# Evacuations issued ahead of side streams, attention jobs over 19 points, and sample heads in bursts of two

## The chip, the cores and the metric

One core of one Trainium2 chip runs the whole program. The metric is the device time of one execution in microseconds; the time before is the median of three runs. A core has TensorE (PE in the profile; its weight loads are PEld), VectorE (DVE), ScalarE (ACT), GpSimd (POOL) and SyncE (SP), each of which works through its own list of instructions in order; semaphores tie the lists together. One profiled execution gives start and length of every instruction.

## What is computed

One layer of a streaming encoder over 640 tokens: 512 of a prompt, and 8 samples of 16 tokens each. The reference, cut to what matters here:

```python
z = x @ w_in                                   # xa | ya | glu | q | three gates
xa, ya, glu, q, gates = split(z)
h = rg_lru(causal_conv4([state_conv_a, xa]))   # sigmoid, exp, sqrt, scan
out_a = (h * gelu(ya)) @ proj_a
u = glu[..., :512] * sigmoid(glu[..., 512:])
v = causal_depthwise_conv31([state_conv_b, u])
out_b = silu(layer_norm(v, over 512 channels)) @ proj_b
out_c = softmax(q k^T / sqrt(128)) v @ proj_c  # 4 heads, 256 memory tokens;
                                               # the samples use cache_mem_k / cache_mem_v
merged = g0 * out_a + g1 * out_b + g2 * out_c  # g = sigmoid(gates)
x = layer_norm(alpha * x + merged @ w_out)
x = layer_norm(alpha * x + (silu(x @ w_ffn_gate) * (x @ w_ffn_up)) @ w_ffn_down)
```

All matrices are float32.

## The kernel before

**Tiling.** Activations lie transposed: channels on the 128 partitions, 640 tokens along the free dimension, handled as two halves of 320 (`HT`). A float32 product is made of three rounded ones: high part by high part, high by low, low by high. So every weight tile is copied by ScalarE into a rounded high part (`wh`), and VectorE subtracts to get the low part (`wl`); activations have `xh`, `xl`, or two `s` tiles made in the same way.

**Steps.** The program is a list of steps (`Step`). One with 8 blocks of the inner dimension is 48 matmuls of 128x320 for one block of 128 output channels; one with 4 blocks (`proj_b`, `proj_c`) is 24. Each writes two PSUM buffers named `pu`, of which there are four, so a step reuses the buffers of an earlier step and has to wait until that step's result has been evacuated (copied, or combined, into SBUF by ScalarE or VectorE: the step's `evac`). Two more, `pv`, serve the side work. The sequence is: keys and values of the memory; GLU gates and values, four blocks of each, with four queries in their middle; eight `xa`; eight of the gate of branch C; eight `proj_c`; then four times two of the gate of branch B and two `proj_b`; eight `ya`; the products of branch A and its gate (`pairs`, through `seven`, which forms sums of blocks first); `w_out`; and the feed-forward part.

**Side streams.** Work that isn't a step is written as generators: `attn` (cross-attention of the prompt, `attn_prompt`, then of the samples, `attn_sample`), `b` (the 31-wide convolution `conv_b_stream`, then the layer norm `ln_b_stream`), `lru`, `a`, and sums for the pairs. `advance` runs pieces of them, and issues more as long as a model of VectorE and ScalarE says that they have less queued than TensorE. Because each engine takes its instructions in the order in which the program issued them, what `advance` has issued stands in front of whatever is issued later.

**The main loop.** Each step's matmuls come in a few groups with a yield behind each. The evacuation of the step before is not issued at once but put in `pending`; at the next step's yields the loop calls `advance` and then `flush`, which issues what is pending (lines 1905 to 1912).

**Attention.** `attn_prompt` lists its jobs (transposes, scores, softmax in two parts, values) at 13 points; a `yield` separates them. `attn_sample` forms the scores of one head at a time (16 matmuls, from the cache tiles `kc`), each at a point of its own; the softmax then multiplies each head by the reciprocal of its row sums (`softmax_end`) before the transposes; the values (32 matmuls a head, tiles `vc`) again come one head at a time, and one copy of 128x512 takes them out. The cache is loaded by DMAs that GpSimd issues (L997).

**GpSimd.** It adds up the four channel blocks for the layer norm of branch B, twice (L782 and L784), and sets to zero the tiles into which the samples' queries (L916) and probabilities (L1032) are written.

**The GLU values.** The first three GLU steps form a group: their first halves of the tokens are done while the last tokens are still being prepared, then the second halves follow (`x_step`). There, in `fm`, the products of one block follow each other: high-high, high-low (which reads `xl`), low-high.

Of the kernel before, what the change touches and what calls it, by code (L numbers as in the profile page):

```python
# [143 lines left out]
def trunk(ctx, tc, x_prompt, x_sample, mem_t, rows_a, rows_b, hist_b, cache_k, cache_v, ln_in_g, ln_in_b, w_in,  # L144
# [484 lines left out]
    def fm(p, w, rh, rl, K, cs=(0, 1), apart=False):  # L629
        hi, lo = w  # L630
        if apart:
            for a, b in ((hi, rh), (hi, rl), (lo, rh)):
                for k in range(K):
                    for c in cs:
                        P.matmul(p[c][:, :HT], a[:, k], b(k, c), start=(k == 0 and a is hi and b is rh),
                                 stop=(k == K - 1 and a is lo))
                yield b is rl
            return
# [27 lines left out]
    def x_step(ld, o, evac, group=None):  # L666

        def mm(w):
# [4 lines left out]
            if group[1][0] is s:  # L673
                until(lambda: {0, 1, 2} <= turned)
                for z, q in enumerate(group[1]):
# [3 lines left out]
                    for n, few in enumerate(fm(q.p, q.w, xrh, xrl, KD, (0,), z in (0, 2))):  # L679
# [6 lines left out]
            yield from fm(s.p, w, xrh, xrl, KD, (1,))  # L686
# [92 lines left out]
    def ln_b_stream():  # L779
        def total(x):  # L780
            y = get([128, T])
            G.tensor_tensor(y, x[0], x[1], op=OP.add)  # L782
            for k in range(2, KC):
                G.tensor_tensor(y, y, x[k], op=OP.add)  # L784
# [91 lines left out]
    def attn_prompt():  # L876
# [35 lines left out]
        def queries(_):  # L912

            qs = qv["s"] = [get([128, NH, 128]) for _ in range(2)]
            for e in range(2):
                G.memset(qs[e], 0.0)  # L916
# [49 lines left out]
        for jobs in (((k_turn, 0),), ((k_split, 0), (scores, 0)), ((soft_a, 0), (scores, 1)), ((soft_b, 0), (soft_a, 1)),  # L966
                     ((turn, 0), (soft_b, 1), (scores, 2)), ((turned_split, 0), (soft_a, 2), (turn, 1)),
                     ((turned_split, 1), (soft_b, 2), (scores, 3)), ((soft_a, 3), (values, 0), (turn, 2)),
                     ((queries, 0), (values_split, 0), (turned_split, 2), (soft_b, 3)), ((turn, 3),),
                     ((turned_split, 3),), ((values, 1),), ((values_split, 1),)):  # L970
# [16 lines left out]
    def attn_sample():  # L987
# [25 lines left out]
        for h in range(NH):  # L1013
            yield None
            scores(h)
            if h + 2 < NH:
                load(kc, cache_k, h + 2)
            if h == NH - 1:
                load(vc, cache_v, 0)
            yield 1  # L1020
        free(*qs)
        pr = softmax_start(acc)
        yield 1
        load(vc, cache_v, 1)
        yield None
        pr = softmax_end(*pr)
        yield 1
        yield None
        pT = [[get([128, 4, 128]) for _ in range(2)] for _ in range(2)]
        for e in range(2):  # L1030
            for i in range(2):
                G.memset(pT[e][i], 0.0)  # L1032
# [11 lines left out]
        for h in range(NH):  # L1044
# [8 lines left out]
            if h + 2 < NH:  # L1053
                load(vc, cache_v, h + 2)
            yield 1
            yield None
# [4 lines left out]
        copy(o, p[:, 0])  # L1061
# [937 lines left out]
```

## Time and profile before

| | us |
|---|---|
| median of three runs (1058.47, 1059.86, 1059.86) | 1059.86 |
| the profiled execution | 1059.77 |
| its span in the profile | 1058.0 |
| PE busy | 1041.5 |
| DVE busy | 801.6 |
| ACT busy | 495.9 |
| POOL busy | 96.0 |

The span is what the profile covers from the first to the last instruction; the 1.8 us between it and the execution's own time lie around it. An engine that is busy 98% of the span, as PE is, isn't necessarily fast all that time: its matmuls are pipelined, and a matmul that starts late, or runs at a lower granted clock, counts as busy. Times of rows are microseconds from the span's start.

### The profile page before, as it was taken

The numbers are of one execution on the slowest core, as the hardware profiler recorded it, in microseconds if no ns is written. First come the engines' busy times: TensorE is split into PE (matmuls) and PEld (weight loads), VectorE is DVE, ScalarE is ACT, GpSimd is POOL, SyncE is SP. The second block draws the span as 40 slices with busy tenths as digits, with TensorE's granted clock in tenths as the row PEclk, the third lists the DMA queues.
The fourth block names the chain that finished last, engine by engine and source line by source line (L and its number), as shares of the span: only waits on it lengthen the run. The fifth ranks groups of instructions, "written<-read, shape, count | busy, mean of one in ns | idle before, by whom it ended". The sixth has DMA issues, their size and how long they took to land.

```text
span 1058.0 us, 16736 instructions
## 1 busy us (share of the span) xinstructions
PE 1041.5 (98%) x6689; PEld 986.7 (93%) x6689; DVE 801.6 (76%) x1400; ACT 495.9 (47%) x892; POOL 96.0 (9%) x164
## 2 busy tenths in 40 slices
PE   9999999999999999999999999999999999999997
PEld 6899899899999999999998899999999999888886
DVE  5769889799566746889586569888888887576775
ACT  5723564345674538555332355444444434434350
POOL 0000313223000000000211210000000000100111
PEclk9999999999999999999999999999999999999999
DMA  9722236512121122212735331222222222833471
GB/s 350 245 88 81 75 112 227 188 42 81 40 97 64 61 80 80 86 40 80 259 140 199 127 114 40 94 106 80 81 80 81 82 99 105 309 136 126 179 278 40
DMA packets 29854, 128.89 MB, mean 122 GB/s; under 512 B 4016, under 2 KB 4848, under 8 KB 19920
## 3 DMA queue, kind: packets, MB, share of 16 engines
q1 hardware_dynamic: 21168, 99.59, 26.5%
q0 software_dynamic: 8608, 28.23, 7.6%
q8 instruction: 52, 0.85, 0.3%
q14 instruction: 26, 0.21, 0.1%
HBM read 115.31 MB, written 12.50 MB: 121 GB/s over the span
## 4 chain that ended last, share of the span: by engine, by line
PE 83%; DVE 9%; ACT 3%; DMA 2%; issue 1%; POOL 0%; SPq 0%; DVEq 0%; ACTq 0%; POOLq 0%
PE pu L64 73%; PE pv L64 9%; DVE s L64 7%; ACT s L64 2%; DVE wl L64 1%; ACT L64 1%; DMA s<-in_w_mem_k 1%; DMA n<-s 1%; DMA s<-in_w_mem_v 1%; DVE xres L64 0%; ACT wh L64 0%; DMA s<-in_x_prompt 0%; DVE mx L64 0%; POOL s L784 0%; DVE xl L64 0%
## 5 line engine op out<-in xcount | busy, mean ns | idle before, releaser
L64 PE MATMUL pu<-xh,wh 128*128 128x320 f32 x1040 | 246.9, 312 | 3.5 <-ACT s L64 2.6
L64 PE MATMUL pu<-xh,wl 128*128 128x320 f32 x1040 | 244.3, 310 | 0.0
L64 ACT ACTIVATE wh<-wr 128x1024 fp32r<-128x1024 f32 (+1 forms) x149 | 134.9, 908 | 231.7 <-PE pu L64 138.7
L64 PE MATMUL pu<-xl,wh 128*128 128x320 f32 x888 | 216.6, 310 | 1.4 <-DVE xl L64 1.4
L64 PE MATMUL pu<-s,wh 128*128 128x320 f32 x1064 | 185.5, 310 | 1.8 <-DVE s L64 1.3
L64 DVE TENSOR_TENSOR s<-s,s 128x640 f32<-128x640 f32 (+5 forms) x200 | 141.8, 728 | 57.1 <-ACT s L64 54.8
L64 PEld LDWEIGHTS pu<-xh,wh 128*128 128x128 f32 x1040 | 176.5, 189 | 7.8 <-ACT s L64 3.8
L64 PEld LDWEIGHTS pu<-xh,wl 128*128 128x128 f32 x1040 | 176.9, 189 | 0.3 <-ACT s L64 0.3
L64 DVE TENSOR_TENSOR wl<-wr,wh 128x1024 fp32r<-128x1024 f32 (+1 forms) x113 | 129.8, 1151 | 62.3 <-ACT wh L64 62.1
L64 PEld LDWEIGHTS pu<-s,wh 128*128 128x128 f32 x1064 | 163.2, 188 | 3.2 <-ACT wh L64 1.1
L64 PEld LDWEIGHTS pu<-xl,wh 128*128 128x128 f32 x888 | 152.9, 189 | 1.8 <-DVE xl L64 1.8
L64 PE MATMUL pu<-s,wl 128*128 128x320 f32 x808 | 146.8, 309 | 0.0
L64 ACT ACTIVATE s<-s 128x640 fp32r<-128x640 f32 (+4 forms) x148 | 89.9, 627 | 96.4 <-DVE s L64 90.1
L64 DVE TENSOR_TENSOR s<-s,pu 128x320 f32<-128x320 f32 x188 | 88.6, 485 | 56.6 <-PE pu L64 52.9
L64 PEld LDWEIGHTS pu<-s,wl 128*128 128x128 f32 x808 | 125.6, 188 | 0.2 <-issue 0.2
L64 DVE SCALAR_TENSOR_TENSOR s<-s,pb,s 128x511 f32<-128x511 f32 (+14 forms) x240 | 114.5, 551 | 9.5 <-ACT s L64 9.4
L64 PE MATMUL pu<-wh,s 128*128 128x512 f32 x364 | 107.0, 383 | 0.0
L64 PEld LDWEIGHTS pu<-wh,s 128*128 128x128 f32 x364 | 66.9, 188 | 13.8 <-ACT wh L64 0.6
L64 ACT ACTIVATE s<-pu 128x320 f32<-128x320 f32 (+2 forms) x90 | 36.6, 441 | 65.3 <-PE pu L64 65.2
L64 PE MATMUL pu<-s,s 128*128 128x512 f32 (+1 forms) x236 | 61.9, 413 | 0.0
L64 PE MATMUL pu<-wl,s 128*128 128x512 f32 x182 | 57.1, 381 | 0.0
L64 PEld LDWEIGHTS pu<-s,s 128*128 128x128 f32 x236 | 43.1, 190 | 14.1 <-issue 7.1
(127 smaller groups left out, 1133.3 us busy)
## 6 DMA issues: line engine op xcount, KB each, us to landing
wr<-in_w_in SPq DMA_DIRECT2D x26, 1024.0 KB, 4.8
wr<-in_w_ffn_down SPq DMA_DIRECT2D x19, 1024.0 KB, 4.9
wr<-in_w_ffn_gate SPq DMA_DIRECT2D x11, 1024.0 KB, 4.8
wr<-in_w_ffn_up SPq DMA_DIRECT2D x11, 1024.0 KB, 4.7
s<-in_cache_k POOLq DMA_DIRECT2D x16, 256.0 KB, 5.6
s<-in_cache_v POOLq DMA_DIRECT2D x16, 256.0 KB, 4.9
wr<-in_proj_a SPq DMA_DIRECT2D x4, 1024.0 KB, 6.7
wr<-in_w_out SPq DMA_DIRECT2D x4, 1024.0 KB, 5.2
```

Source lines behind the costliest of these rows:

```text
L64: return f(*a, **k)
```

## The change

It has six parts.

1. **The main loop** calls `flush` before `advance`: a finished step's evacuation is issued before side work at the same yield.
2. **`attn_prompt`** spreads the same jobs over 19 points.
3. **`attn_sample`**: two heads' scores at one point, and two heads' values at one point; the loads of the cache move with them. The probabilities are no longer multiplied by the reciprocals; the copy of the result takes each head's reciprocal as its scale, in four pieces of 128x128.
4. **GpSimd to VectorE**: the block sums of `ln_b_stream`, and the memsets of the queries and probabilities.
5. **`fm`** gets a second order for a step that is done in turns: all high-high products, then all low-high ones of the weights, then those that need `xl`. The first step of the group uses it for its second half of tokens.
6. **`seven`**: the first pair forms the sums for the product `s1` at its second step instead of right before that product.

```diff
-    def fm(p, w, rh, rl, K, cs=(0, 1), apart=False):
+    def fm(p, w, rh, rl, K, cs=(0, 1), apart=None):
         hi, lo = w
         if apart:
-            for a, b in ((hi, rh), (hi, rl), (lo, rh)):
+            turns = ((hi, rh), (hi, rl), (lo, rh)) if apart == "w" else ((hi, rh), (lo, rh), (hi, rl))
+            for i, (a, b) in enumerate(turns):
                 for k in range(K):
                     for c in cs:
-                        P.matmul(p[c][:, :HT], a[:, k], b(k, c), start=(k == 0 and a is hi and b is rh),
-                                 stop=(k == K - 1 and a is lo))
-                yield b is rl
+                        P.matmul(p[c][:, :HT], a[:, k], b(k, c), start=(k == 0 and i == 0), stop=(k == K - 1 and i == 2))
+                yield i == 1
...
-                    for n, few in enumerate(fm(q.p, q.w, xrh, xrl, KD, (0,), z in (0, 2))):
+                    for n, few in enumerate(fm(q.p, q.w, xrh, xrl, KD, (0,), "w" if z in (0, 2) else None)):
...
-            yield from fm(s.p, w, xrh, xrl, KD, (1,))
+            yield from fm(s.p, w, xrh, xrl, KD, (1,), "x" if s is group[1][0] else None)
...
     def ln_b_stream():
         def total(x):
             y = get([128, T])
-            G.tensor_tensor(y, x[0], x[1], op=OP.add)
+            V.tensor_tensor(y, x[0], x[1], op=OP.add)
             for k in range(2, KC):
-                G.tensor_tensor(y, y, x[k], op=OP.add)
+                V.tensor_tensor(y, y, x[k], op=OP.add)
...
-                G.memset(qs[e], 0.0)
+                V.memset(qs[e], 0.0)
...
-        for jobs in (((k_turn, 0),), ((k_split, 0), (scores, 0)), ((soft_a, 0), (scores, 1)), ((soft_b, 0), (soft_a, 1)),
-                     ((turn, 0), (soft_b, 1), (scores, 2)), ((turned_split, 0), (soft_a, 2), (turn, 1)),
...
+        for jobs in (((k_turn, 0),), ((k_split, 0),), ((scores, 0),), ((soft_a, 0), (scores, 1)), ((soft_b, 0), (soft_a, 1)),
+                     ((turn, 0),), ((turned_split, 0), (soft_b, 1), (scores, 2)), ((soft_a, 2),), ((turn, 1),),
...
     def attn_sample():
-        for h in range(NH):
-            yield None
-            scores(h)
-            if h + 2 < NH:
-                load(kc, cache_k, h + 2)
-            if h == NH - 1:
-                load(vc, cache_v, 0)
+        for h in range(0, NH, 2):
+            for _ in range(2 if h else 1):
+                yield None
+            for i in range(2):
+                scores(h + i)
+            for i in range(2):
+                if h == 0:
+                    load(kc, cache_k, h + 2 + i)
+                elif i >= 0:
+                    load(vc, cache_v, i - 0)
             yield 1
         free(*qs)
-        pr = softmax_start(acc)
+        pr, sm = softmax_start(acc)
         yield 1
-        load(vc, cache_v, 1)
+        rc = small.tile([128, NH], F32, name="rc")
+        V.reciprocal(rc, sm)
         yield None
-        pr = softmax_end(*pr)
-        yield 1
+        yield None
         yield None
         pT = [[get([128, 4, 128]) for _ in range(2)] for _ in range(2)]
...
-                G.memset(pT[e][i], 0.0)
+                V.memset(pT[e][i], 0.0)
...
             free(*vc[h])
-            if h + 2 < NH:
-                load(vc, cache_v, h + 2)
-            yield 1
-            yield None
+            if h % 2:
+                if h == 1:
+                    load(vc, cache_v, 2)
+                    load(vc, cache_v, 3)
+                yield 1
+                for _ in range(2 if h == 1 else 1):
+                    yield None
...
-        copy(o, p[:, 0])
+        for h in range(NH):
+            hs = slice(h * 128, (h + 1) * 128)
+            A.activation(o[:, hs], p[:, 0, hs], AF.Copy, scale=rc[:, h:h + 1])
...
-            if first and xn[0] == "s":
+            if first and i == 1:
+                before = lambda: sums_for("s1")
+            elif first and xn[0] == "s":
                 before = lambda xn=xn: sums_for(xn)
...
             while new and s.wait:
                 new.pop(0).prep_lo()
+            flush()
             advance()
-            flush()
             while new:
                 new.pop(0).prep_lo()
```

Where the instructions stand now, at three places. The rows are a list of ScalarE's instructions in program order: operation, output, input and shape; `x2` is the same row twice. The number at the end of a name tells tiles apart, and differs between the two programs.

First, ScalarE from the middle of the GLU steps on, before. `s_83_1310<-pu` is the evacuation of the last GLU gate; `pv,nm` are the exponentials of a softmax (`soft_a`), `rc` its division (`soft_b`), `wh` the weights of a later step.

```order
L64 ACTIVATE wh<-wr 128x1024
L64 ACTIVATE s_78_1231<-s_78_1231,rc 128x256 x2
L64 ACTIVATE s_79_1232<-s_79_1232,rc 128x256 x2
L64 ACTIVATE s_81_1300,sm<-pv,nm 128x256 x2
L64 ACTIVATE s_82_1301,sm<-pv,nm 128x256 x2
L64 ACT_TABLE_LOAD
L64 ACTIVATE s_83_1310<-pu 128x320 x2
L64 ACTIVATE wh<-wr 128x1024
```

The same place of the changed program, where that evacuation is `s_81_1289<-pu`:

```order
L64 ACTIVATE wh<-wr 128x1024
L64 ACT_TABLE_LOAD
L64 ACTIVATE s_81_1289<-pu 128x320 x2
L64 ACTIVATE s_79_1237<-s_79_1237,rc 128x256 x2
L64 ACTIVATE s_80_1238<-s_80_1238,rc 128x256 x2
L64 ACT_TABLE_LOAD
L64 ACTIVATE s_82_1303,sm<-pv,nm 128x256 x2
L64 ACTIVATE s_83_1304,sm<-pv,nm 128x256 x2
L64 ACTIVATE wh<-wr 128x1024
```

The evacuation, with the table load that belongs to it, now stands ahead of both softmax pieces, and a second table load ahead of the exponentials.

Second, ScalarE at the first two steps of the gate of branch B, before. `lru` marks the exponentials of the recurrence, the row behind each pair is a square; `pu,pa` are the sigmoids that evacuate a gate's step; `s_190_2988<-s_190_2988` is the first of four square roots.

```order
L64 ACTIVATE s_216_3525<-s_211_3370,lru_88 128x640
L64 ACTIVATE s_211_3370<-s_211_3370,lru_88 128x640
L64 ACTIVATE s_192_3011<-s_216_3525 128x640
L64 ACTIVATE wh<-wr 128x512
L64 ACT_TABLE_LOAD
L64 ACTIVATE s_217_3561<-pu,pa 128x320 x2
L64 ACT_TABLE_LOAD
L64 ACTIVATE s_190_2988<-s_190_2988 128x640
```

The same of the changed program:

```order
L64 ACT_TABLE_LOAD
L64 ACTIVATE s_215_3547<-pu,pa 128x320 x2
L64 ACT_TABLE_LOAD
L64 ACTIVATE s_216_3565<-s_203_3326,lru_88 128x640
L64 ACTIVATE s_203_3326<-s_203_3326,lru_88 128x640
L64 ACTIVATE s_181_2900<-s_216_3565 128x640
L64 ACTIVATE wh<-wr 128x1024
L64 ACT_TABLE_LOAD
L64 ACTIVATE s_217_3585<-pu,pa 128x320 x2
```

The sigmoids now stand between groups of exponentials, with a table load on each side, where they stood behind all of them. Over the whole program ScalarE has 24 table loads instead of 21.

Third, ScalarE at the samples' softmax, before; `s_151_2374<-pu` evacuates an `xa` step.

```order
L64 ACTIVATE s_140_2300<-s_83_1310,pb 128x640
L64 ACTIVATE wh<-wr 128x1024
L64 ACTIVATE s_145_2354,sm<-pv,nm 128x256 x2
L64 ACTIVATE s_146_2355,sm<-pv,nm 128x256 x2
L64 ACTIVATE s_151_2374<-pu 128x320 x2
```

The same of the changed program:

```order
L64 ACTIVATE s_141_2328<-s_81_1289,pb 128x640
L64 ACTIVATE s_150_2398,sm<-pv,nm 128x256 x2
L64 ACTIVATE s_151_2399,sm<-pv,nm 128x256 x2
L64 ACTIVATE wh<-wr 128x1024
L64 ACT_TABLE_LOAD
L64 ACTIVATE s_152_2441<-pu,pa 128x320 x2
```

The exponentials used to stand directly ahead of the evacuation of an `xa` step; now they stand, with a weight copy and a table load, ahead of the evacuation of the first step of the gate of branch C (`pu,pa`), and the multiplication by `rc` that followed them is gone: it is in the four copies behind the values.

More of the change, by code (lines that the diff above doesn't have):

```diff
@@ L965, in attn_prompt @@
         matmuls = (k_turn, scores, turn, values)
-        for jobs in (((k_turn, 0),), ((k_split, 0), (scores, 0)), ((soft_a, 0), (scores, 1)), ((soft_b, 0), (soft_a, 1)),
-                     ((turn, 0), (soft_b, 1), (scores, 2)), ((turned_split, 0), (soft_a, 2), (turn, 1)),
-                     ((turned_split, 1), (soft_b, 2), (scores, 3)), ((soft_a, 3), (values, 0), (turn, 2)),
-                     ((queries, 0), (values_split, 0), (turned_split, 2), (soft_b, 3)), ((turn, 3),),
-                     ((turned_split, 3),), ((values, 1),), ((values_split, 1),)):
+        for jobs in (((k_turn, 0),), ((k_split, 0),), ((scores, 0),), ((soft_a, 0), (scores, 1)), ((soft_b, 0), (soft_a, 1)),
+                     ((turn, 0),), ((turned_split, 0), (soft_b, 1), (scores, 2)), ((soft_a, 2),), ((turn, 1),),
+                     ((turned_split, 1), (soft_b, 2), (scores, 3)), ((soft_a, 3),), ((values, 0),),
+                     ((values_split, 0), (soft_b, 3), (turn, 2)), ((turned_split, 2),), ((turn, 3), (queries, 0)),
+                     ((turned_split, 3),), (), ((values, 1),), ((values_split, 1),)):
             for f, i in jobs:
```

## Prediction

> **What bounds the kernel now.** I read the page first: busy shares and the chain that ended last.
>
> ```profile
> span 1058.0 us, 16736 instructions
> PE 1041.5 (98%) x6689; PEld 986.7 (93%) x6689; DVE 801.6 (76%) x1400; ACT 495.9 (47%) x892; POOL 96.0 (9%) x164
> PE 83%; DVE 9%; ACT 3%; DMA 2%; issue 1%; POOL 0%; SPq 0%; DVEq 0%; ACTq 0%; POOLq 0%
> ```
>
> TensorE is busy 98% of the span and is 83% of the chain. The change leaves its set of matmuls as it is, so time can be won only where TensorE stands still, starts late, or runs at a lower clock. Next, the table of waits, for PE alone (what waited, for whom, us in total, times, longest).
>
> ```profile
> PE pu L64 <- ACT s L64: 3.1, 3, 2.4
> ...
> PE pu L64 <- DVE xl L64: 1.4, 2, 0.9
> PE pu L64 <- DVE s L64: 1.3, 2, 0.9
> ...
> PE pv L64 <- POOL s L784: 0.3, 1, 0.3
> ```
>
> So the waits are few and short, and none of them is for a DMA of weights once the start is over. [...] The PE timeline folds runs of equal matmuls into a row (start, length, count); here are the rows around each stall in reach of the change, in order of time.
>
> ```profile
> 47.09 0.41 PE L64 MATMUL pu<-xh,wh 128*128 128x320 f32 x1
> 48.43 0.41 PE L64 MATMUL pu<-xl,wh 128*128 128x320 f32 x1 [0.93 <-DVE xl L64]
> ...
> 118.43 0.46 PE L64 MATMUL pu<-xl,wh 128*128 128x320 f32 x2
> 118.72 0.46 PE L64 MATMUL pu<-xh,wl 128*128 128x320 f32 x2
> 121.60 0.74 PE L64 MATMUL pu<-xh,wh 128*128 128x320 f32 x2 [2.42 <-ACT s L64]
> ...
> 123.06 0.58 PE L64 MATMUL pu<-xl,wh 128*128 128x320 f32 x2
> ...
> 126.64 0.46 PE L64 MATMUL pu<-xh,wl 128*128 128x320 f32 x2
> ...
> 191.60 0.46 PE L64 MATMUL pu<-xh,wl 128*128 128x320 f32 x2
> 191.98 1.07 PE L64 MATMUL pv<-s,s 128*32 128x256 f32 x16
> 192.99 0.56 PE L64 MATMUL pu<-xh,wh 128*128 128x320 f32 x2
> ...
> 210.45 0.46 PE L64 MATMUL pu<-xh,wl 128*128 128x320 f32 x2
> 211.13 0.74 PE L64 MATMUL pu<-xh,wh 128*128 128x320 f32 x2 [0.22 <-ACT s L64]
> ...
> 248.94 0.46 PE L64 MATMUL pu<-xh,wl 128*128 128x320 f32 x2
> 249.69 1.13 PE L64 MATMUL pv<-s,ones 128*128 128x512 f32 x2 [0.29 <-POOL s L784]
> ...
> 288.44 0.46 PE L64 MATMUL pu<-s,wl 128*128 128x320 f32 x2
> 289.78 1.02 PE L64 MATMUL pu<-s,wh 128*128 128x320 f32 x4 [0.89 <-DVE s L64]
> ...
> 345.19 0.46 PE L64 MATMUL pu<-s,wl 128*128 128x320 f32 x2
> 346.11 1.12 PE L64 MATMUL pu<-s,wh 128*128 128x320 f32 x4 [0.46 <-ACT s L64]
> ...
> 395.47 0.46 PE L64 MATMUL pu<-s,wl 128*128 128x320 f32 x2
> 396.36 1.11 PE L64 MATMUL pu<-s,wh 128*128 128x320 f32 x4 [0.43 <-DVE s L64]
> ...
> 464.68 0.31 PE L64 MATMUL pu<-xl,wh 128*128 128x320 f32 x1
> 465.75 0.41 PE L64 MATMUL pu<-xh,wh 128*128 128x320 f32 x1 [0.75 <-ACT xh L64]
> 466.61 0.41 PE L64 MATMUL pu<-xl,wh 128*128 128x320 f32 x1 [0.45 <-DVE xl L64]
> 466.86 0.31 PE L64 MATMUL pu<-xh,wh 128*128 128x320 f32 x1
> ```
>
> Undisturbed, two matmuls take 118.72 - 118.43 = 0.29 us, 147 ns each; a full step of 48 is then 7.05 us, one of 24 is 3.53. A row of two lasts 0.46, of four 0.46 + 0.29 = 0.75. A stall is the gap beyond that spacing, plus what the first row behind it lasts too long.
>
> **The change part by part.** The sum is made against the profiled execution, 1059.77 us (span 1058.0 and 1.8 around it), which is 0.1 under the median of 1059.86.
>
> *Second order in `fm`.* 48.43 - 47.09 - 0.15 = 1.2 us, and 0.1 on the restart: 1.3. With the new order 16 matmuls, 2.35 us, stand ahead of the first that reads `xl`, which came 1.2 too late. Won: **1.3**.
>
> *Evacuation of the last GLU gate.* 121.60 - 118.72 - 0.29 = 2.6, and 0.74 - 0.46 = 0.3 on the restart. Behind it the matmuls are slow: from 123.06 to 126.64 seven rows of two take 3.58 instead of 2.05, 1.5 more. The stretch from 123 to 127 shows why (third from the end, PEclk, the granted clock):
>
> ```profile
> 119.81 1.28 ACT L64 ACT_TABLE_LOAD   x1
> 121.11 0.77 ACT L64 ACTIVATE s<-pu 128x320 f32<-128x320 f32 x2
> ...
> 123.00:127.00 4.00, 4.00 (x19) 4.00 (x18) 4.00 (x9) 1.41 (x4) 0.00 (x0) 0.57 0.02 4
> ```
>
> The clock fell to 0.57 after the gap. ScalarE's rows show the cause: the copy out of `pu` starts at 121.11, behind two softmax pieces and a table load. In the new order it stands ahead of them. Table load and copy, about 2.1 us, and the weight copy ahead of them (1.1) then end some 3.2 us behind their step, and the next user of the buffers comes a step, 7.05, later. Won: **4.4**.
>
> [...] A clock loss that stays, for whatever cause, has 1 in 10 and gives 1050.4, inside the forecast's range.
>
> *Sample softmax.* 211.13 - 210.45 - 0.29 + 0.28 = 0.7: four exponentials stood ahead of an evacuation. Now they come behind the second burst of scores, ahead of another evacuation, so a new deadline has to be met. These are its terms:
>
> ```profile
> 207.29 1.23 DVE L64 TENSOR_REDUCE mx<-pv 128x4 f32<-128x1024 f32 x1 [6.81 <-PE pv L64]
> L64 ACT ACTIVATE s<-pv,nm 128x256 f32<-128x256 f32 x20 | 9.2, 474 | 14.6 <-DVE nm L64 13.7 <-issue 0.9
> L64 ACT ACTIVATE wh<-wr 128x1024 fp32r<-128x1024 f32 x97 | 102.3, 1059 | 198.3 <-PE pu L64 108.2 <-issue 45.0 <-PE pv L64 23.7
> L64 ACT ACTIVATE s<-pu,pa 128x320 f32<-128x320 f32 x36 | 17.1, 520 | 2.5 <-PE pu L64 2.4
> ```
>
> Maximum 1.2 and its sign 0.2, four exponentials 1.9, weight copy 1.06, table load 1.28, two sigmoids 1.0: 6.6 us behind the burst, against a step of 7.05. It just fits. Won: **0.7**; at the other end it comes back.
>
> *Bursts of two.* Entry to a burst costs 191.98 - 191.60 - 0.29 = 0.09, leaving it 0.56 - 0.46 = 0.10, and the pipe's change of shape inside the burst something that no row separates. Four bursts fewer are 0.8 at least, 1.3 if the inside is worth as much as the two edges seen and a little; I take the middle, **1.0**. The cache loads, four DMAs a head on POOL's queue, move with the bursts; those for the next pair of heads have more than a whole step of 7 us before their burst, so I count nothing; a miss would cost one stop like the 0.7 above. The division that moves into the copy takes four pieces from ScalarE ahead of the transposes, and splits one copy in four behind the values; both lie beside steps, and count nothing.
>
> *Block sums and memsets on VectorE.* The matmuls with `ones` wait for GpSimd: 249.69 - 248.94 - 0.29 = 0.46, and about 0.1 on the restart.
>
> ```profile
> 246.53 3.10 POOL L784 TENSOR_TENSOR s<-s,s 128x640 f32<-128x640 f32 x1 [15.41 <-DVE s L64]
> L64 DVE TENSOR_TENSOR s<-s,s 128x640 f32<-128x640 f32 x56 | 45.7, 820 | 3.2 <-ACT s L64 2.3
> ```
>
> The last addition took GpSimd 3.10 us; the same shape takes VectorE 0.82, so the sum is there 2.3 earlier. Six of them are 4.9 us of VectorE's time, the six memsets of 128x512 at most as much again (no row shows one there; I take 0.4 each, half of the nearest row, which reads two operands of 640). VectorE, busy 76%, has the room: what hides them is its idle time. The price if that cover is gone is one addition in front of an evacuation, 0.82. Won: **0.5**.
>
> *`flush` ahead of `advance`, later stages.* `proj_c`: 289.78 - 288.44 - 0.29 + 0.27 = 1.3. First `proj_b` of a later pair: 346.11 - 345.19 - 0.29 + 0.37 = 1.0. Next to the last: 396.36 - 395.47 - 0.29 + 0.36 = 1.0. In all three a combined or copied result stood behind side work, which now stands behind it. Steps of 3.53 us leave less room than those of 7.05, so I count 0.4 as lost again at each of the first two: 1.3 + 1.0 + 1.0 - 0.8 = **2.5**.
>
> *The price of it.* In the gate of branch B sigmoids now stand between exponentials, with three more table loads there. The tightest: when a gate's second step ends, ScalarE has a weight copy 1.06, a table load 1.28 and the two sigmoids, 0.95, in all 3.3, while one `proj_b` step of 3.53 runs; the next step needs the buffers. That is 0.2 us to spare, at a handful of places. I take three misses of 0.4 with restart: **-1.2**; bounds: none, and three stops like that at 345 and 395, 3.0.
>
> [...] The trace has the next activation at 121.11, 0.02 behind the load's end: no drain there.
>
> *Sums for the first pair.* From 464.68 to 466.86 three matmuls take 2.18 instead of 0.44: they wait for the copy and the low part of one sum. Formed at the second step, both come earlier. Won: **1.7**.
>
> Sum: 1.3 + 4.4 + 0.7 + 1.0 + 0.5 + 2.5 - 1.2 + 1.7 = 10.9, and 1059.8 - 10.9 = **1048.9**.
>
> **Rivals.** *The later half is given back* (3 in 10). The five early terms, 7.9 us, stay; in the stages with short steps the table loads between sigmoids and exponentials produce as much waiting as `flush` takes away, up to one stop with a loss of clock like that at 121.60 (4.4). Against it: the deadlines above hold on paper. For it: by 0.2 us only. Between 1059.8 - 7.9 = 1051.9 and 1056.3. The table load's drain, as a mechanism of these rows, belongs here, with 1 in 20.
>
> *No change* (7 in 100). Stops vanish and others of the same length come, because something else paces TensorE: 1059.8. Against it: with 98% busy nothing else in the waits is steady, and the early stops have names.
>
> *Slower* (6 in 100). A single mechanism: each sigmoid between exponentials waits for a square and an exponential that themselves wait for VectorE's convolutions. If that chain ends later than the deadline by over 2.4 us, each such place costs the stop and the clock, 4.4; three table pairs there and one at the sample softmax make 17.6, against 10.9 + 1.2 won: 1059.8 + 5.5 = 1065.3. It decides from the fourth such place on, since three are 13.2.
>
> **How the numbers follow.** Forecast 57 in 100, 1045.5 to 1051.5: its low end is all terms at their best bound (10.9 + 1.2 + 0.8 + 0.3 = 13.2, 1046.6) and a little for stops not counted; 30 in 100 for the rival up to 1056.3. The range, 1045.5 to 1055.5, leaves out no change, slower, and the end of the first rival. A measurement of this kernel can tell 0.2%, 2.1 us, from no change: faster means under 1057.7. That gives 0.87, 0.07 and 0.06.
>
> **What would show it.** In the new profile: no wait of PE for `xl` near 47; no stop and no clock under 1 near 119; no row of POOL ahead of `pv<-s,ones`; no wait for `xh` near 454; and PE's waits for ACT in the gate of branch B under 0.5 us each. The prediction is wrong if PE stops for over a microsecond in short steps, or if matmuls away from any stop are spaced wider than 147 ns.

## The result and the profile after

| | before | changed |
|---|---|---|
| median, us | 1059.86 (1058.42 to 1061.69, 5 runs) | 1047.70 (1047.46 to 1048.17, 5 runs) |
| profiled execution | 1059.77 | 1048.17 |
| span | 1058.0 | 1046.4 |

The ratio is 0.9888, with a 95% interval of 0.9874 to 0.9903: 1.1% faster. The page of the changed kernel:

```profile
span 1046.4 us, 16741 instructions
PE 1034.9 (99%) x6689; PEld 984.0 (94%) x6689; DVE 801.9 (77%) x1412; ACT 499.2 (48%) x894; POOL 83.8 (8%) x152
PE 92%; DVE 3%; ACT 2%; DMA 2%; issue 1%; SPq 0%; DVEq 0%; POOL 0%; ACTq 0%
```

TensorE's share of the chain rose from 83% to 92%, and VectorE's fell from 9% to 3%: less of the end is set by somebody whom TensorE waits for. VectorE and ScalarE do as much as before. The table of PE's waits, whole:

```profile
PE pu L64 <- DVE ident L64: 1.4, 1, 1.4
PE pu L64 <- DVE wh L64: 0.6, 1, 0.6
PE pu L64 <- ACT xh L64: 0.5, 1, 0.5
PE pu L64 <- DMA s<-in_w_mem_k: 0.5, 2, 0.3
PE pu L64 <- DVE s L64: 0.5, 2, 0.2
PE pv L64 <- DVE xres L64: 0.4, 1, 0.4
```

The 3.1 us for `ACT s` are gone, and so are those for `xl` and for GpSimd. The wait for `wh` is new; the kernel before waited for an `xh` too (0.8 us), but near 464, in the first pair. Where the waits are now, the PE timeline shows (start, length, matmuls in the row):

```profile
47.33 0.86 PE L64 MATMUL pu<-xh,wh 128*128 128x320 f32 x4
48.74 0.85 PE L64 MATMUL pu<-xh,wh 128*128 128x320 f32 x4 [0.55 <-ACT xh L64]
...
194.45 1.93 PE L64 MATMUL pv<-s,s 128*32 128x256 f32 x32
...
249.42 0.46 PE L64 MATMUL pu<-xh,wl 128*128 128x320 f32 x2
249.71 1.24 PE L64 MATMUL pv<-s,ones 128*128 128x512 f32 x4
...
454.13 0.31 PE L64 MATMUL pu<-xl,wh 128*128 128x320 f32 x1
454.99 0.86 PE L64 MATMUL pu<-xh,wh 128*128 128x320 f32 x4 [0.55 <-DVE wh L64]
456.08 0.67 PE L64 MATMUL pu<-s,wl 128*128 128x320 f32 x3 [0.23 <-DVE s L64]
...
647.19 2.21 PE L64 MATMUL pu<-s,wh 128*128 128x320 f32 x12
649.63 0.53 PE L64 MATMUL pu<-s,wl 128*128 128x320 f32 x2 [0.24 <-DVE s L64]
```

Near 47 a smaller stop is left, for another tile than before. The `ones` follow 0.29 behind the row ahead of them, without a stop. Near 454 two smaller stops are left, and near 649 there is one that the kernel before did not have.

To see where each microsecond came from, compare when the same matmul, counted from the first, starts in either trace; both have 6689, mostly in the same order. The lead is the time before less the time after.

| matmul | before, us | after, us | lead | gained since the row above, and the place |
|---|---|---|---|---|
| 180 | 42.51 | 42.76 | -0.25 | the start, not touched |
| 240 | 52.50 | 52.37 | 0.13 | 0.4: second half of the GLU group |
| 660 | 113.15 | 113.00 | 0.15 | 0.0 |
| 780 | 134.53 | 129.99 | 4.54 | 4.4: last GLU gate |
| 1920 | 281.44 | 274.31 | 7.13 | 2.6: samples' attention and `ones` |
| 1980 | 291.66 | 283.11 | 8.54 | 1.4: `proj_c` |
| 2400 | 354.26 | 344.71 | 9.55 | 1.0: a first `proj_b` |
| 2760 | 408.66 | 397.51 | 11.15 | 1.6: the last `proj_b` and the first `ya` |
| 3240 | 481.10 | 469.21 | 11.90 | 0.8: first pair |
| 4320 | 657.46 | 645.57 | 11.89 | 0.0 |
| 4380 | 666.42 | 655.13 | 11.29 | -0.6: pairs of the feed-forward part |
| 6420 | 1000.69 | 989.08 | 11.61 | 0.3: last part, not touched |

That is the whole difference of the two profiled executions, 1059.77 - 1048.17 = 11.6. In the row of matmul 2760, 0.7 of the 1.6 is a late start that the prediction doesn't list; in the kernel before it is

```profile
399.94 0.46 PE L64 MATMUL pu<-s,wl 128*128 128x320 f32 x2
400.50 0.84 PE L64 MATMUL pu<-xh,wh 128*128 128x320 f32 x2
```

where the second row would start at 400.23 without a wait and last 0.46.

### The profile page after: what moved, and what is told of

Its sections match the earlier page's. It is cut to its first block, busy times and chain, and to the rows that moved or that the text cites. A ratio compares the mean times of both kernels' runs of the same rounds, so it can differ in the third digit from the quotient of the medians.

```text
span 1046.4 us, 16741 instructions
## 1 busy us (share of the span) xinstructions
PE 1034.9 (99%) x6689; PEld 984.0 (94%) x6689; DVE 801.9 (77%) x1412; ACT 499.2 (48%) x894; POOL 83.8 (8%) x152
## 4 chain that ended last, share of the span: by engine, by line
PE 92%; DVE 3%; ACT 2%; DMA 2%; issue 1%; SPq 0%; DVEq 0%; POOL 0%; ACTq 0%
PE pu L64 82%; PE pv L64 10%; DVE s L64 1%; ACT s L64 1%; DVE wl L64 1%; DMA s<-in_w_mem_v 1%; DMA s<-in_w_mem_k 0%; DMA s<-in_x_prompt 0%; DVE xres L64 0%; ACT wh L64 0%; ACT xh L64 0%; DVE wh L64 0%; DVE st L64 0%; DVE xl L64 0%; ACT L64 0%
## 5 line engine op out<-in xcount | busy, mean ns | idle before, releaser
L64 PE MATMUL pu<-xh,wh 128*128 128x320 f32 x1040 | 243.0, 310 | 1.1 <-DVE wh L64 0.6
L64 PE MATMUL pu<-xh,wl 128*128 128x320 f32 x1040 | 241.2, 309 | 0.0
L64 PE MATMUL pu<-xl,wh 128*128 128x320 f32 x888 | 213.5, 309 | 0.0
L64 DVE TENSOR_TENSOR s<-s,s 128x640 f32<-128x640 f32 (+5 forms) x206 | 144.8, 722 | 52.6 <-ACT s L64 50.0
L64 DVE SCALAR_TENSOR_TENSOR s<-s,pb,s 128x511 f32<-128x511 f32 (+14 forms) x240 | 112.1, 539 | 2.9 <-ACT s L64 2.9
```

The lines of the kernel that those rows point to most:

```text
L64: return f(*a, **k)
```

## The experiments

Each was timed beside the kernel of before on the same chip, whose median was then between 1058.5 and 1059.6. "Over" means over the changed kernel's 1047.70, which was timed in another session. As the median of before moved by up to 1.4 us between the sessions, a difference of about 1 us or less is read from the traces, by the starts of the same matmuls, and not from the medians.

**The loop's order, taken back.**

```diff
+            advance()
             flush()
-            advance()
```

> The changed kernel with `advance` ahead of `flush` again, all else changed. Theory, the parts pay singly where the profile of before shows their stop: only the three stages with short steps come back (1.3 at proj_c, 1.0 at the first proj_b of a pair, 1.0 + 0.6 at the last ones), the stop behind the last GLU gate stays away because its cure is the attention list; some 3.5 us over the changed kernel's 1047.7, about 1051. Rival, the loop's order is what cured every evacuation, the GLU one too: 8 us over, about 1056, with PEclk under 1 near 119.

Measured: 1069.30 (1068.88 to 1069.44), 21.6 over, and slower than the kernel of before: ratio 1.0096 (1.0081 to 1.0111). Both theories fall on the size. Stops in the later stages came back, longer than before (1.84 us at 318.7), and there was no stop near 119; but over 8 us were lost in one place that neither had named, the start of `proj_a`, where TensorE stopped for 1.83 us behind 511.9 and the granted clock was 0.50 from 516.32 to 526.56, which alone can cost up to 5 us (an estimate, half of these 10.24 us):

```profile
511.80 0.46 PE L64 MATMUL pu<-s,wl 128*128 128x320 f32 x2
514.09 0.55 PE L64 MATMUL pu<-s,wh 128*128 128x320 f32 x2 [1.83 <-ACT s L64]
```

The experiment with single heads, below, shows what that is.

**The loop's order alone**, in the kernel of before.

```diff
+            flush()
             advance()
-            flush()
```

> The kernel of before with `flush` ahead of `advance` and nothing else. Theory: the late stops go (3.9 us), the GLU stop with its loss of clock stays, some new late work in the feed-forward part (0.6) comes: about 1056.5. Rival: the GLU stop goes too, about 1052.

Measured: 1052.70 (1052.04 to 1053.32), 6.9 under the 1059.56 of before there. The rival was nearer: the stop near 119 is gone although the attention list is the old one. The exponentials that stood ahead of the evacuation start at 115.41 instead of 117.86, so the evacuation comes in time though it still stands behind them. In exchange the transposes of probabilities wait 1.3 us for ScalarE near 138.

**13 points again.** The list of jobs of `attn_prompt` as before, all else changed.

```diff
-        for jobs in (((k_turn, 0),), ((k_split, 0),), ((scores, 0),), ((soft_a, 0), (scores, 1)), ...
+        for jobs in (((k_turn, 0),), ((k_split, 0), (scores, 0)), ((soft_a, 0), (scores, 1)), ...
```

> The changed kernel with the prompt's attention jobs at 13 points again. Theory: the evacuation of the last GLU gate stands behind soft_b 0 and soft_a 1 again, TensorE stops 2.6 us near 119 and the granted clock falls: 4.4 us over, about 1052. Rival, the loop's order alone cures it: 1047.7 within 0.5.

Measured: 1051.63 (1051.60 to 1051.85), 3.9 over. The size is the theory's, the place isn't: there is no stop near 119. TensorE stops near 138 instead (1.2 us for ScalarE's softmax), and twice near the sample heads (1.0 and 0.4). So the stop near 119 has two cures, either of which is enough, and what the 19 points bring on top is that no transpose or value waits for its softmax.

**Single heads again.** `attn_sample` as before but for its memsets, all else changed.

```diff
-        for h in range(0, NH, 2):
-            for _ in range(2 if h else 1):
-                yield None
-            for i in range(2):
-                scores(h + i)
+        for h in range(NH):
+            yield None
+            scores(h)
...
+        pr = softmax_end(*pr)
```

> The changed kernel with the samples' attention of before (one head at a point, division ahead of the transposes), memsets still on VectorE. Theory: four more bursts (1.0 to 1.4) and the 0.7 at the softmax come back, about 1049.6. Rival, bursts cost only their two edges of 0.1 and the new loop order already cures the softmax: 0.8 us over, 1048.5.

Measured: 1064.36 (1064.09 to 1064.65), 16.7 over. Neither the theory nor the rival holds. Counted by the starts of the same matmuls, about 1 us of it is lost at the heads, 1 more up to the pairs, 3 at the first pair, and 11 around the start of `proj_a`, where the granted clock is 0.50 for 13.65 us, which can make up to 6 of the 11 (an estimate, half of TensorE's 12.37 busy us there). That place, PE and then ScalarE:

```profile
505.06 0.46 PE L64 MATMUL pu<-s,wl 128*128 128x320 f32 x2
509.21 1.76 PE L64 MATMUL pu<-s,wh 128*128 128x320 f32 x4 [3.70 <-ACT s L64]
```

```profile
507.03 1.06 ACT L64 ACTIVATE wh<-wr 128x1024 fp32r<-128x1024 f32 x1 [5.12 <-DMA wr<-in_proj_a]
507.99 0.55 ACT L64 ACTIVATE s<-s,pa 128x320 f32<-128x320 f32 x1
508.44 0.72 ACT L64 ACTIVATE s<-s 128x640 fp32r<-128x640 f32 x1
510.79 0.74 ACT L64 ACTIVATE s<-s 128x640 fp32r<-128x640 f32 x1 [1.63 <-DVE s L64]
```

The copies of 128x640 to `fp32r` split the operands of `proj_a`, the recurrence's output. Here they stand behind a weight copy that waits for its DMA. The changed kernel's ScalarE waits 4.30 us for the same DMA, and nothing stops, because by then it has split the operands that the next matmuls read. How late the recurrence is, the view of the tile `hout` tells (ScalarE's copies into it; the last are the final states). The changed kernel:

```profile
L64 ACT ACTIVATE hout<-s x32: 186/202/231, 137.1 to 438.5; 128x3 f32<-128x3 f32 x8, 128x24 f32<-128x24 f32 x8, 128x1 f32<-128x1 f32 x8, 128x8 f32<-128x8 f32 x8
```

With single heads:

```profile
L64 ACT ACTIVATE hout<-s x32: 188/202/232, 136.9 to 488.7; 128x3 f32<-128x3 f32 x8, 128x24 f32<-128x24 f32 x8, 128x1 f32<-128x1 f32 x8, 128x8 f32<-128x8 f32 x8
```

The last copy starts 50 us later, though the sample heads ended only 4.6 us later (236.0 against 231.4). The last exponential of the recurrence is 16 us late (429.9 against 414.0); the rest is added behind that, where the recurrence shares VectorE and ScalarE with the sums for the pairs; which of them holds it up was not traced. With the old loop order the last copy is at 494.0.

**Both attention parts as before.** The two edits above together: 13 points and single heads.

> The changed kernel with both parts of the attention as before (13 points, single heads), all else changed. In the kernel with 19 points and single heads the recurrence's last copy came at 488.7 instead of 438.5 and proj_a's operands were late by 10 us. Theory, what counts there is how many points the attention takes before the recurrence can go on: with 13 points the delay is gone, no stop at the start of proj_a, about 1052 (4 us for the heads and for the softmax waits near 138). Rival, single heads are late by themselves: the stop near 505 stays, about 1062.

Measured: 1051.15 (1050.97 to 1051.57), 3.5 over. The theory holds: taking back both costs far less than taking back the heads alone (16.7), and no more than the list alone (3.9; the two are not told apart). The last copy of the recurrence is at 441.3, and there is no stop at `proj_a`. So single heads are harmless with 13 points and cost 16.7 with 19: the bursts of two are what pays for the six added points. That the longer attention holds up everything queued behind it fits this, and in the kernel with 19 points and single heads the matmuls with `ones` come 24 matmuls later too (matmul 1776 instead of 1752); the way from there to the 50 us was not traced.

**The old order of products.**

```diff
-            yield from fm(s.p, w, xrh, xrl, KD, (1,), "x" if s is group[1][0] else None)
+            yield from fm(s.p, w, xrh, xrl, KD, (1,))
```

> The changed kernel with the old order of products in the group's second half of tokens. Theory from the trace of after (the stop near 47 only shrank, from 1.3 to 0.8, because the copy `xh` of the last tokens is as late as `xl` almost): 0.4 to 0.5 us over the changed kernel. Rival, the forecast's step: 1.3 us over.

Measured: 1048.19 (1047.92 to 1048.49), 0.5 over, which the medians alone don't tell from nothing (ratio 0.9894, 0.9879 to 0.9910, against 0.9888). The trace has the theory's size: the matmul behind the stop starts 1.34 us after the last ahead of it, 0.86 us in the changed kernel, and by the starts 0.4 us are lost there. The rival's 1.3 is refuted.

**Sums on GpSimd.**

```diff
-            V.tensor_tensor(y, x[0], x[1], op=OP.add)
+            G.tensor_tensor(y, x[0], x[1], op=OP.add)
...
-                V.tensor_tensor(y, y, x[k], op=OP.add)
+                G.tensor_tensor(y, y, x[k], op=OP.add)
```

> The changed kernel with the block sums of branch B on GpSimd again. Theory: the matmuls with `ones` wait for GpSimd again, 0.5 us over. Rival, VectorE's 4.9 us less of work pays elsewhere, or the sums have time now: 0.

Measured: 1054.37 (1053.14 to 1056.17), 6.7 over: thirteen times the theory's half microsecond. PE, then the windows ahead of and behind the restart (third from the end is PEclk):

```profile
245.25 0.46 PE L64 MATMUL pu<-xh,wl 128*128 128x320 f32 x2
249.31 2.07 PE L64 MATMUL pv<-s,ones 128*128 128x512 f32 x2 [3.60 <-POOL s L784]
```

```profile
245.40:249.30 3.90, 0.31 (x3) 0.04 (x1) 3.90 (x6) 2.38 (x4) 2.00 (x1) 0.83 0.00 0
249.30:251.50 2.20, 2.19 (x5) 1.16 (x5) 2.20 (x4) 0.00 (x0) 0.00 (x0) 0.50 0.15 22
```

One more thing differs besides the engine. The `ones` are matmul 1728 here and 1752 in the changed kernel, 24 matmuls or 3.5 us earlier: the model by which `advance` issues work counts VectorE's time but not GpSimd's, so the stream goes on as if the sums cost nothing. The next experiment separates the two.

**GpSimd, but everything at its place.** The sums' price is still added to VectorE's modelled time.

```diff
-            V.tensor_tensor(y, x[0], x[1], op=OP.add)
+            G.tensor_tensor(y, x[0], x[1], op=OP.add)
+            V.time += V.price(V, "tensor_tensor", (y,), {})
...
-                V.tensor_tensor(y, y, x[k], op=OP.add)
+                G.tensor_tensor(y, y, x[k], op=OP.add)
+                V.time += V.price(V, "tensor_tensor", (y,), {})
```

> The changed kernel with the block sums on GpSimd, but their price still counted as VectorE's in the model by which `advance` issues work, so that every other instruction stays at its place (in the kernel with the sums on GpSimd and uncounted, the matmuls with `ones` stand at matmul 1728 instead of 1752). Theory, the place was what cost there: the last addition runs from 245.1 to 247.1 or 248.2, the matmuls come at 249.7, no stop, within 0.5 of the changed kernel's 1047.7. Rival, GpSimd's speed is what cost: a stop of 3.6 near 249 and loss of clock, about 1054.

Measured: 1050.95 (1050.11 to 1052.07), 3.3 over: between the two (two runs kept a granted clock of 0.998 or more, 1050.11 and 1050.30, and two had 0.996, 1051.59 and 1052.07; by the trace, one of the former, it is 2.1). All matmuls stand at their places in the changed kernel's order, so the place was half of the 6.7 or more, and the `ones` now wait for nothing. But TensorE stops for 1.77 us at 245.8, for an evacuation, because VectorE is 2.4 us late. The reason is 20 us earlier. GpSimd's additions there, and VectorE's two groups of convolution beside them:

```profile
222.41 1.94 POOL L782 TENSOR_TENSOR s<-s,s 128x640 f32<-128x640 f32 x1 [14.04 <-PE pv L64]
224.43 2.62 POOL L785 TENSOR_TENSOR s<-s,s 128x640 f32<-128x640 f32 x1
```

```profile
220.49 4.01 DVE L64 SCALAR_TENSOR_TENSOR s<-s,pb,s 128x499 f32<-128x499 f32 x6
224.43 1.21 DVE L64 TENSOR_TENSOR wl<-wr,wh 128x1024 fp32r<-128x1024 f32 x1
225.56 5.01 DVE L64 SCALAR_TENSOR_TENSOR s<-s,pb,s 128x496 f32<-128x496 f32 x8
```

The same groups of the changed kernel, with no GpSimd beside them:

```profile
220.71 2.69 DVE L64 SCALAR_TENSOR_TENSOR s<-s,pb,s 128x499 f32<-128x499 f32 x6
223.32 1.22 DVE L64 TENSOR_TENSOR wl<-wr,wh 128x1024 fp32r<-128x1024 f32 x1
224.45 3.72 DVE L64 SCALAR_TENSOR_TENSOR s<-s,pb,s 128x496 f32<-128x496 f32 x8
```

1.3 us more for each of the two additions. In each group a single instruction took it all: 1.66 instead of 0.35, and 2.03 instead of 0.73, and each ended only behind GpSimd's addition (by 0.1 and 0.5 us). Beside each of the other four additions of this run a VectorE instruction lasted longer too: over the six it is 0.8 to 1.4 us each, 7.4 in all, where VectorE does the six itself in 4.9. So the six additions that GpSimd took "off" VectorE went with more of VectorE's time than doing them takes. In the kernel before it was the same (0.4 to 1.4 each, 6.6 in all), which is most of why VectorE's busy time rose by only 0.3 us, from 801.6 to 801.9, although it took over six additions and six memsets of 0.48 us.

**Sums for `s1` late again.**

```diff
-            if first and i == 1:
-                before = lambda: sums_for("s1")
-            elif first and xn[0] == "s":
+            if first and xn[0] == "s":
```

> The changed kernel with the sums for `s1` formed right before its product again. Theory: the wait for the copy and the low part returns, 1.7 instead of the 1.1 that the changed kernel still stops there: 0.7 us over. Rival, the forecast's step: 1.7 us over.

Measured: 1049.61 (1048.89 to 1050.50), 1.9 over, with a span only 0.7 longer than the changed kernel's; the two stops near 454 are 1.0 longer than there by the starts of the matmuls. By the trace the theory is right, and its 0.7 somewhat small; the median, whose runs spread over 1.6 us, is nearer to the rival, but it mixes two kinds of runs: 1048.89 (the traced one) and 1049.12 with a granted clock of 0.998 or more over the whole span, 1050.09 and 1050.50 with 0.996. The first two are 1.2 and 1.4 over; the other two have the lower clock over the span (the experiment on stops and the clock, below, has the same of the kernel before). The step of the forecast as such, a wait of 1.7 that goes whole, is refuted by the stops that the changed kernel still has.

**The thin margin.** The sigmoids that evacuate the second step of branch B's gate are issued twice, the second time past the model.

```diff
-                each(A.activation, g, p, AF.Sigmoid, bias=pa[:, j, 8 + br:9 + br])
+                for z in range(2 if (br, j) == (1, 1) else 1):
+                    each((A.engine if z else A).activation, g, p, AF.Sigmoid, bias=pa[:, j, 8 + br:9 + br])
```

> The changed kernel with the two sigmoids of the second step of branch B's gate issued twice: 0.9 us more on ScalarE in the chain for which 0.2 us to spare was reckoned; all else in the same order. Theory, that margin is what it was reckoned: TensorE stops there for 0.6 to 0.7 and 0.3 on the restart, some 0.9 us over. Rival, the buffers are needed later than reckoned: no stop, 0.

Measured: 1048.43 (1048.26 to 1048.89), 0.7 over by the median and 0.55 by the trace. ScalarE's chain in the changed kernel, as reckoned:

```profile
312.21 1.06 ACT L64 ACTIVATE wh<-wr 128x1024 fp32r<-128x1024 f32 x1 [0.52 <-PE pu L64]
313.28 1.28 ACT L64 ACT_TABLE_LOAD   x1
314.58 0.94 ACT L64 ACTIVATE s<-pu,pa 128x320 f32<-128x320 f32 x2
```

It ends at 315.52, and the step that needs the buffers starts at 315.82: the margin was there. PE in the experiment:

```profile
315.31 0.46 PE L64 MATMUL pu<-s,wl 128*128 128x320 f32 x2
315.77 1.13 PE L64 MATMUL pu<-s,wh 128*128 128x320 f32 x4
316.74 0.45 PE L64 MATMUL pu<-s,wl 128*128 128x320 f32 x2
```

From 315.31 to 316.74 six matmuls take 1.43 instead of 0.88: 0.55 lost for 0.8 us more on ScalarE. The theory holds, somewhat smaller: the repeated pair of sigmoids, one for each of the two buffers, runs from 315.19 to 316.14, and the first of the matmuls already starts at 315.77.

**Stops and the clock.** Sigmoids of four steps of branch C's gate repeated.

```diff
-                each(A.activation, g, p, AF.Sigmoid, bias=pa[:, j, 8 + br:9 + br])
+                for z in range({1: 8, 3: 9, 5: 10, 7: 11}.get(j, 1) if br == 2 else 1):
+                    each((A.engine if z else A).activation, g, p, AF.Sigmoid, bias=pa[:, j, 8 + br:9 + br])
```

> The changed kernel with the sigmoids that evacuate steps 1, 3, 5 and 7 of branch C's gate issued 8, 9, 10 and 11 times, so that TensorE stops there for some 0.5, 1.3, 2.1 and 3.0 us; the order of everything else stays. Theory from the stops seen so far (1.78 us kept the clock once, 1.84 and 2.42 lost it): the granted clock stays at 1.00 behind the first two, and falls to 0.5 for 3 to 4 us, some 2 us after the restart, behind the last two; 6.9 of stops, 1.2 of restarts and 3.4 of clock, about 1059. [...]

Measured, in one run: 1056.04. Only two stops came, since most of the repeated sigmoids fitted into the step: 3.03 us ahead of 238.3, and 1.63 ahead of 280.8. The windows of the longer one, then of the shorter:

```profile
235.00:238.30 3.30, 0.30 (x3) 0.04 (x1) 3.30 (x8) 3.30 (x11) 0.00 (x0) 0.89 0.40 169
238.30:241.30 3.00, 2.97 (x12) 2.74 (x13) 3.00 (x6) 1.54 (x7) 0.00 (x0) 0.50 0.00 0
```

```profile
279.00:280.80 1.80, 0.21 (x2) 0.00 (x0) 1.27 (x2) 1.80 (x4) 0.00 (x0) 1.00 0.00 0
280.80:282.80 2.00, 1.96 (x15) 1.99 (x16) 2.00 (x6) 1.10 (x2) 0.00 (x0) 1.00 0.00 0
```

With two of the four stops, the time decides nothing; the clock does. Of the theory, 1.00 behind the shorter stop and the loss behind the longer one came, but not its time: the clock fell at 237.56, 0.8 us ahead of the restart, and stayed at 0.50 until 244.39, for 6.83 us.

In the kernel before, the clock was 0.50 from 123.23 to 126.64, which is 3.41 us; with the loop's old order from 321.76 to 325.18 and from 516.32 to 526.56, with single heads from 508.20 to 521.85, with the sums on GpSimd (uncounted) from 247.94 to 254.77. These five stretches and that of this run are 3.41, 3.42, 6.83 (twice), 10.24 and 13.65 us long, about one, two, three or four times 3.41. They did not begin at one distance from the restart: in the kernel before 1.63 us behind it (121.60), here 0.8 ahead of it. The stops that were measured, by length:

| idle of PE | 0.99 | 1.33 | 1.63 | 1.77 | 1.78 | 1.84 | 2.42 | 3.03 | 3.60 | 3.70 |
|---|---|---|---|---|---|---|---|---|---|---|
| lowest clock behind it | 1.00 | 1.00 | 1.00 | 1.00 | 1.00 | 0.50 | 0.50 | 0.50 | 0.50 | 0.50 |

In these ten, the stops up to 1.78 us kept the clock and those from 1.84 lost it. The stop of 1.83 at the start of `proj_a` is not among them, since shorter ones follow it: from 514.10 to 516.50 TensorE was busy for 1.44 of 2.40 us, and the clock was lost at 516.32.

The runs without a trace speak against taking 1.8 us for a threshold. The kernel before, timed 37 times beside the experiments, has a granted clock of 0.998 over the whole span in 12 runs, of 1057.88 to 1058.53 us, and of 0.996 or 0.997 in 25 runs, of 1059.13 to 1060.18. One stretch of 3.41 us at half clock is 1.7 us, or 0.0016 of the span, so by this estimate the same stop of 2.42 us kept the clock in a third of the runs. The stop of 1.77, with the sums on GpSimd at their place, likewise goes with 0.998 or more in two runs and with 0.996 in two. That it was these stops in the untraced runs is inferred, since these left only their time and their granted clock; and what decides whether such a stop costs clock, no run shows.

**Two edits to the stops that are left.** The first four blocks' products that don't need the late half of `xh` come first, and the feed-forward part has the old loop order.

```diff
+            halves = [range(K)] if apart == "w" else [range(K // 2), range(K // 2, K)]
+            order = [(i, ks) for ks in halves for i in range(3)]
+            if apart == "x":
+                order = [(i, ks) for ks in halves for i in range(2)] + [(2, range(K))]
...
+            if i < first["ffn"]:
+                flush()
+                advance()
+            else:
+                advance()
+                flush()
```

> The changed kernel with two edits at the stops that it still has: in the group's second half the first four blocks' high-high and low-high products come ahead of the last four blocks' (whose `xh` is late), and in the feed-forward part `advance` comes ahead of `flush` again. Theory: the stop near 47 shrinks from 0.8 by 0.6, the one near 649 (0.6) goes: 1.1 us under the changed kernel, about 1046.6. Rival, the stops move elsewhere in the feed-forward part: 1047.7 within 0.4.

Measured: 1047.04 (1046.89 to 1047.22), profiled span 1045.1 against 1046.4. The PE timeline near 47:

```profile
47.02 0.86 PE L64 MATMUL pu<-xh,wh 128*128 128x320 f32 x4
47.72 0.75 PE L64 MATMUL pu<-xh,wl 128*128 128x320 f32 x4
48.43 0.86 PE L64 MATMUL pu<-xh,wh 128*128 128x320 f32 x4
49.12 0.75 PE L64 MATMUL pu<-xh,wl 128*128 128x320 f32 x4
```

No wait is left there, and the one near 649 is gone too. By the starts of the matmuls the first edit won 0.6 and the second 0.4 us; behind both the kernel leads the changed one by 1.3 us, 0.3 of it from the start, which the edits don't touch. By the ratios, 0.9891 (0.9875 to 0.9908) against 0.9888, the two kernels are not told apart, since they were timed in different sessions and before varied by 1.4 us between these. Both stops are gone; that this is worth its 1 us in the median is not shown.

## Why the prediction was right

It was 1048.9, in a range of 1045.5 to 1055.5; measured were 1047.7. Term by term, with the leads:

- **GLU gate, 4.4: 4.4.** Stop, restart and the clock behind it went together. The cause given, an evacuation behind softmax pieces, was right. That the clock's 1.5 came in full hangs on the traced run of before, which had lost it; 12 of that kernel's 37 other runs have a granted clock of 0.998 and seem to have kept it. Which part cures it was not asked in the prediction; both the loop's order and the list do.
- **Second order in `fm`, 1.3: 0.4.** The step said that 16 matmuls stand ahead of the first that reads `xl`, and took `xl` for the only late tile. But the last four blocks of `xh` are as late: eight high-high products can't run ahead, only four. The wait for `xl` was what ended last, not what came next.
- **Softmax, bursts and `ones`, 0.7 + 1.0 + 0.5 = 2.2: 2.6 together.** The step with the new deadline (6.6 against 7.05) held: there is no stop at that place. The bursts were the term put too low: each of the eight bursts of before cost 1.2 us with both its edges, 9.6 in all, and the four of double length cost 2.06 to 2.08 each, 8.3 in all, so four bursts fewer saved 1.3, the upper of the two values that the prediction weighed: 0.33 a burst, where its two edges were 0.19 by the prediction's rows. For the sums, 0.5 is what the stop of before had cost; in the new order GpSimd would have cost 3.3 at the same place and 6.7 at its own. What the prediction priced as VectorE's burden, 4.9 us for six additions, was made up for: beside GpSimd's additions VectorE had lost 6.6.
- **Later stages, 2.5, and the price in the gate of branch B, -1.2: 4.0 together.** All three stops went whole, and with them a fourth, near 400, that the prediction had not listed (0.7 of the 1.6 in that row of leads). The price was the mis-sized term: the reckoned margin of 0.2 us was really there, once the chain is timed (0.3), and nothing was late. Three misses had been charged for a place that was merely close, and so had 0.8 as lost again at the first two stops. Of the drain of a table load, to which the prediction gave 1 in 20, no run shows one: in the timed chain the sigmoids start at 314.58, 0.02 behind the load's end.
- **First pair, 1.7: 0.8.** The wait for the sum went; a low part of weights, which VectorE writes into a tile named `wh`, is next late, behind sums of weights on the same engine. "What is late next" wasn't asked in this step.
- **Not foreseen, -0.6**: the stop near 649. There `flush` puts a table load and an evacuation (627.35 to 629.41) ahead of a split copy for which VectorE idles 1.69 us, and VectorE, which works through a long list of sums, is late twenty microseconds later. That the one makes the other was followed only so far, but taking the loop's order back in that part took the stop away.

The losses, 0.9 at `fm`, 0.9 at the first pair and 0.6, and the gains, 2.7 and 0.4, leave 0.7: 11.6 by the profiled executions instead of 10.9. By the medians it is 12.2. So the places and mechanisms were right in the main, while the closeness of the total is in part luck: 2.4 us too much and 3.1 too little nearly cancel. The total also hangs on the granted clock of the runs of before: those with 0.998 have a median of 1058.2, 10.5 above the changed kernel, and the others 1059.65, 12.0 above it.

The signs that the prediction named came, two of them by the letter only: there is no wait for `xl` near 47 and none for `xh` near 454, but another tile is waited for at both places.

The rival "the later half is given back" speaks of stages with table loads between sigmoids: it didn't come, by 0.3 us at the place that was timed. The experiment with 0.8 us more on ScalarE shows that a stop begins there once the margin is used up (0.55 lost); losses of the rival's size were not produced. The slower rival had the wrong mechanism: with single heads, side work that is late pays at `proj_a`, at 505 us, not in the gate of branch B. That it lay so near, one part of the change away, the prediction did not see.

What the prediction assumed throughout, that the parts add up, is what the runs contradict. Taken back one at a time (the memsets stayed on VectorE throughout) they cost 21.6, 3.9, 16.7, 0.5, 6.7 and 1.9 us, 51 in all, where the whole change brought 12.2; the loop's order alone brought 6.9.

## What to carry to other kernels

Where one engine is busy 98%, list its late starts one by one from its timeline, and cost a change at each, with the restart and the clock behind it; then ask at each place what is late next. Parts that reorder side work aren't additive: a list with more points needs something that shortens it elsewhere, and work that is late need not be paid for until the first stage that reads its result. Work that a scheduling model doesn't count (here GpSimd's) is issued as if it were free, and whoever waits for it then stands too early. Before two medians are compared over a microsecond, compare the granted clocks of their runs: the kernel before had 0.998 in 12 of its 37 runs and 0.996 or 0.997 in the other 25, with medians of 1058.2 and 1059.65 us.

## What the runs showed of the hardware

- The granted clock was 0.50 in six stretches at stops, of 3.41 us (kernel before, from 123.23; 3.42 with the loop's old order, from 321.76) or about two, three or four times that: 6.83 (sums on GpSimd, uncounted, from 247.94; repeated sigmoids, from 237.56), 10.24 (loop's old order, from 516.32) and 13.65 (single heads, from 508.20). In the ten stops of the table it was 0.50 behind those of 1.84 to 3.70 us and stayed at 1.00 behind those of 0.99 to 1.78. The length of a stop alone doesn't seem to decide: by the granted clocks of its runs, the kernel before, with the same stop of 2.42, seems to have kept the clock in 12 of 37 (0.998) and lost it in 25 (0.996 or 0.997).
- Beside each of the six additions of 128x640 on GpSimd, in the run where they stand at their place, a VectorE instruction lasted 0.8 to 1.4 us longer than in the changed kernel, 7.4 in all; in the kernel before 0.4 to 1.4, 6.6 in all.
- The first matmuls behind a stop lasted 0.1 to 0.4 us longer than elsewhere, even where the clock stayed at 1.00: near 47 in the kernel before one lasted 0.41 instead of 0.31, and behind the stop of 1.77 us a row of two lasted 0.83 instead of 0.46.
